# Interleaving the first two projection sections of a decoder layer by row blocks

## Chip, cores, metric

One Trainium2 chip, one core. The metric is the device time of one execution in microseconds (us), as the median of several runs. The names of the engines follow the profile: PE is TensorE (its weight loads are PEld), ACT is ScalarE, DVE is VectorE, POOL is GpSimd, SP is SyncE, which issues most of the transfers.

## What is computed

A decoder layer over 256 rows of width 1,024 in float32: a norm, one wide projection, two attention mixers, a gated merge, a feed-forward part and a last norm. The change touches the projection's first two column groups and the compression that reads them:

```python
h = rmsnorm(x, norm1_g[layer])
proj = h @ w_in[layer]
q_n = proj[..., :OFF_KV]
kv_n = proj[..., OFF_KV:OFF_GN]
...
k_c, v_c, k_s, v_s, k_w, v_w = (kv[:, :, i] for i in range(6))
...
kc = compress_blocks(k_c, cmp_pe_k[layer], cmp_k_w1[layer], cmp_k_w2[layer])
vc = compress_blocks(v_c, cmp_pe_v[layer], cmp_v_w1[layer], cmp_v_w2[layer])
...
def compress_blocks(k, pe, w1, w2):
    kb = k[:, idx] + pe[None, None, :, None, :]
    kb = jnp.transpose(kb, (0, 3, 1, 2, 4)).reshape(b, g, n_cmp, CMP_BLOCK * d)
    return jax.nn.gelu(kb @ w1) @ w2
```

The row factor of `rmsnorm` (one number for each row) is applied after the matmul, when its result is copied out of PSUM; only the gain is applied to x before it.

## The kernel before

**Weights in parts.** Each float32 matmul is made of three faster ones. A weight chunk is loaded into `raw`, ACT writes its rounded copy `whi` (`split`, line 114), DVE the remainder `wlo` (line 116); x times the gain is split the same way into `hTh` (line 187) and `hTl` (line 193). `mm3` gives the three matmuls whi x hTh, wlo x hTh and whi x hTl (all through `mm`, line 238).

**Chunks and sections.** The projection is cut into sections: kva (384 columns; chunks 0 and 1), kvb (408 columns; chunks 2 and 3), then q, qm, km and vm with 512 columns each (chunks 4 to 11), then the gates. A chunk holds four row blocks of 128 of the 1,024 rows of the weight, so a section is two chunks, eight row blocks, with two results (rows 0 to 127 and 128 to 255 of x): 48 matmuls. The pool `wp` holds three `raw`, three `whi` and three `wlo` tiles, so the load of a chunk waits until DVE has read an older one.

**Order.** The program is written in the order in which each engine executes it. `run_slot` emits a half section's matmuls; `at(pos, f, ...)` puts other work between them, at a fraction `pos` of the list. An engine works its own list strictly in order, so what is emitted earlier is also waited for first.

**The start.** kva's first chunk comes in four pieces of one row block (192 KB), three on ACT's queue and one on SP's, the second in two pieces; kvb's chunks come whole (816 KB). x comes in five pieces on SP's queue (`x_part`). A loop over the eight row blocks does `hTh`, `hTl` and `split` for kva. Then kva runs (row block by row block), and kvb after it (chunk 2: all blocks of the first result, then of the second).

**Row norm.** `row_squares` (ACT, line 204) and `row_sums` (DVE, line 207) square x and add it up near the end of kva; `row_norm` sums over partitions with four small matmuls into `tp`, DVE makes `stat` (line 213), POOL the power `rstd` (line 214). It stands in the first half of kvb, at 0.9.

**The compression's chain.** kva's results are copied out with the row factor into `kcd` and `kva` (lines 304 and 307); `cmp_gather` transposes `kcd` on PE (line 372, eight transposes) and `gather_evac` adds the positions into `kE` on DVE (line 384, eight operations), both in kvb's second half. Then follow in the q section `rope` on `kva`, `cmp_mlp1` (PE, reads `w1`), `cmp_sum` (with `gl` on ACT and DVE) and `cmp_mlp2`.

Of the kernel before, what the change touches and what calls it, by code (L numbers as in the profile page):

```python
# [8 lines left out]
F32 = mybir.dt.float32  # L9
# [36 lines left out]
def hybrid_layer(ctx: ExitStack, tc: tile.TileContext, gxd, w, w1c, small, const, gf, out):  # L46
# [39 lines left out]


    raw, hi, lo = {}, {}, {}

# [29 lines left out]


    ident = cp.tile([128, 128], F32, name="ident")
    mhalf = cp.tile([128, 4], F32, name="mhalf")
# [10 lines left out]
    gx = cp.tile([128, 16 + 2048], F32, name="gx")  # L133
    raw_tile(0)
    raw_tile(1)

# [3 lines left out]

    for k in range(3):
        load_part(0, k, 4, 1, nc.scalar)
    for a, b in ((0, 1), (1, 2), (2, 4)):
        x_part(a, b)
    load_part(0, 3, 4)
    for a in (4, 6):
        x_part(a, a + 2)
        load_part(1, a % 4, 4, 2)
    load(2)

# [10 lines left out]
    xT = gx[:, 16:].rearrange("p (k q) -> p k q", k=8)  # L161
    load(3)
    nc.sync.dma_start(sm, small)
    nc.sync.dma_start(kc_, const)
    load(4)
    g1, g2 = gx[:, 0:8], gx[:, 8:16]
# [18 lines left out]

    for kt in range(8):
        act.activation(hTh[:, kt, :], xT[:, kt, :], AF.Copy, scale=g1[:, kt:kt + 1])
        if kt == 0:
            hi[0] = wp.tile([128, 2048], F32R, name="whi")
            lo[0] = wp.tile([128, 2048], F32R, name="wlo")  # L190
            dve.tensor_copy(hi[0][:, 0:384], raw[0][:, 0:384])
            split(0, 0, 4, "l")
        dve.scalar_tensor_tensor(hTl[:, kt, :], xT[:, kt, :], g1[:, kt:kt + 1],
                                 hTh[:, kt, :].bitcast(F32), op0=ALU.mult, op1=ALU.subtract)
        if kt:
            split(kt // 4, kt % 4, 4)

    stat = cp.tile([128, 8], F32, name="stat")
    rstd = cp.tile([128, 2], F32, name="rstd")
    hrstd = stat[:, 4:6]  # L200

    def row_squares(i):
# [48 lines left out]
    def xstat(c, n, accs, kts):  # L251

        r = []
        h, l = hi[c], lo[c]
        order = [(t, k) for t in range(2) for k in range(4)]
        if c < 2:
            order.sort(key=lambda e: e[1])
        for t, k in order:
            kt = kts[k]
            if True:  # L260
                lh, ll = (a[:, kt, t * 128:(t + 1) * 128] for a in (hTh, hTl))
                r += mm3(accs[t][:, :n], lh, ll, h[:, k * n:(k + 1) * n],
                         l[:, k * n:(k + 1) * n], kt == 0, kt == 7)
        return r
# [34 lines left out]
    vm = ap_.tile([128, 2, 512], F32, name="vm")  # L299
    tm = {"kva": kva, "kvb": kvb, "vm": vm}  # L300

    def evac_tm(sec, t, acc, n):
        if sec == "kva":
            act.activation(kcd[:, t], acc[:, 0:256].rearrange("p (a d) -> p a d", a=4)[:, :, None, :]
                           .to_broadcast([128, 4, 2, 64]), AF.Copy, scale=rstd[:, t:t + 1])
            acc, n = acc[:, 256:384], 128
        act.activation(tm[sec][:, t, :], acc[:, :n], AF.Copy, scale=rstd[:, t:t + 1])
# [81 lines left out]
    def cmp_mlp1():  # L389
# [5 lines left out]
        act.activation(raw1, tp[:, 0:64], AF.Copy)  # L395
        dve.tensor_reduce(gsum, ident.rearrange("p (g i) -> p i g", g=4), op=ALU.add, axis=AX)

# [190 lines left out]
    def unit_events(s):  # L588
# [15 lines left out]
        if d > 0:  # L604
            at(0.12, d_yevac, d - 1)


    groups = [("kva", 0, 384), ("kvb", C_KVB, 408), ("q", C_Q, 512), ("qm", C_QM, 512),
              ("km", C_KM, 512), ("vm", C_VM, 512)]
    for sec, c0, n in groups:  # L610
        if sec in ("q", "qm", "km"):
            tm[sec] = ap_.tile([128, 2, 512], F32, name="qtm", bufs=2)
        if sec in ("kvb", "q"):
            accs = [ps_e.tile([128, 512], F32, name=f"{sec}acc{t}") for t in range(2)]
        else:
            accs = [acc_tile(), acc_tile()]
        for i in range(2):
            c = c0 + i
            if c == 0:
                at(0.6, load, 5)  # L620
            elif c == 1:
                at(0.88, row_squares, 0)
                for k in range(4):
                    at(0.89, split, 2, k, 4)
                for k in range(1, 4):
                    at(1.1, row_squares, k)
                at(1.1, row_sums, 0, 2, 2)
                at(1.1, row_sums, 4, 6, 2)
                at(1.1, row_sums, 0, 4, 2)
                at(1.1, row_sums, 0, 1, 1)  # L630
                for k in range(4):
                    at(1.2, split, 3, k, 4, "h")
                for k in range(2):
                    at(1.3, split, 3, k, 4, "l")

            elif c == 2:
                at(0.9, row_norm)
                for k in range(2, 4):
                    at(0.91, split, 3, k, 4, "l")
                at(0.92, load, 6)  # L640
                at(0.92, nc.sync.dma_start, w1, w1c)
            elif c == 3:
                for k in range(2):
                    at(0.0, split, 4, k, 2, "h")
                for t in range(2):
                    at(0.01, evac_tm, "kva", t, first[t], 384)
                for k in range(2):
                    at(0.1, split, 4, k, 2, "l")
                at(0.11, load, 7)
                at(0.66, cmp_gather)  # L650
                for k in range(2):
                    at(0.66, gather_evac, k)
                for k in range(2):
                    at(0.7, split, 5, k, 2, "h")
            elif c == 4:
                for t in range(2):
                    at(0.0, evac_tm, "kvb", t, second[t], 408)
                at(0.1, split, 5, 0, 2, "l")
                at(0.2, rope, kva, 2)
                at(0.3, split, 5, 1, 2, "l")  # L660
                at(0.35, load, 8)
                split_events(c, (0.5, 0.55), (0.8, 0.9))
                at(0.7, cmp_mlp1)
            else:
                std_events(c)
            unit_events(c)
            if c == 5:
                at(0.05, gate_evac)
                at(0.09, cmp_sum)
                at(0.1, transp_k, kva, tuple(a[:, 0:1] for a in kswT))  # L670
                at(0.1, rope, kvb[:, :, 0:128], 2)
                at(0.75, cmp_mlp2)
                at(0.75, transp_k, kvb[:, :, 0:128], tuple(a[:, 1:2] for a in kswT))
            if c == 6:
                at(0.45, transp_heads, tm["q"], qT, 0, 1)
                at(0.6, rope, tm["q"], 8)
# [11 lines left out]
            if c == 11:  # L688
                turn["tp"] = ["tp"]
                at(0.09, transp_heads, tm["km"], kmT, 0)  # L690
                at(0.48, transp_heads, tm["km"], kmT, 1)
            if c == 1:
                first = accs
            elif c == 3:
                second = accs
            elif i == 1:
                at(0.49 if sec == "vm" else 0.5, evac_tm, sec, 0, accs[0], n)
# [258 lines left out]
    P = {}  # L956
# [263 lines left out]
```

## Time and profile before

| | |
|---|---|
| median of the timed runs | 370.55 us (369.96, 370.55, 370.82) |
| the profiled execution | 371.17 us |
| its span (first to last instruction) | 369.4 us |
| granted PE clock | 0.998 |
| PE busy | 360.8 us, 98% of the span, 2,387 matmul records |
| DVE busy / ACT busy | 311.6 us (84%) / 234.2 us (63%) |
| transfers | 66.28 MB, 179 GB/s in the mean |

The profile is of one execution. A row of a timeline gives the start, the busy time, the engine, the line of the program, the operation, out<-in by the names of the tiles, the shape, how many were merged into the row, and in brackets how long the engine stood idle before it and what released it. A row of transfers gives the destination and source, the queue, how many, the size of each and the median time from issue to landing in us. A stretch's row gives from:to and length, then the busy time of PE, PEld, DVE, ACT and POOL with their instructions, the PE clock, the share of the DMA engines and GB/s.

### The profile page before, as it was taken

To read this page: it belongs to the slowest core of one execution; us is meant where nothing else is said; L and a number is where in the kernel's file an instruction comes from. 1 tells how busy PE (TensorE), PEld (TensorE's weight loads), DVE (VectorE), ACT (ScalarE), POOL (GpSimd) and SP (SyncE) were. 2 spreads that over 40 slices of the span, in tenths; PEclk is the share of its full clock that TensorE was granted. 3 is DMA by queue.
4 is the path that set the end of the run, shared out by engine and by line. 5 is a ranking of instruction groups with operands and counts; after the bars stand their busy time and mean duration, and the time that the engine had idled before them with its cause. 6 is when DMAs were issued, how large, how long until landed. Compare 5 with 4: busy or idle time off the path is not lost.

```text
span 369.4 us, 5952 instructions
## 1 busy us (share of the span) xinstructions
PE 360.8 (98%) x2387; PEld 318.5 (86%) x2387; DVE 311.6 (84%) x454; ACT 234.2 (63%) x353; POOL 3.7 (1%) x15
## 2 busy tenths in 40 slices
PE   8999999999999999999999999999999999999993
PEld 6987778877778888788999999999999999999983
DVE  4988879896967769766878999999999999995875
ACT  5984364757747667525465888876766677764522
POOL 1010000000000000000000000000000000000000
PEclk9999999999999999999999999999999999999999
DMA  8987436333533334533583655444565566544003
GB/s 265 398 317 295 138 111 227 114 115 114 172 148 137 115 114 137 206 115 114 178 333 119 229 227 220 171 185 184 184 213 215 227 230 227 221 177 174 0 0 114
DMA packets 11402, 66.28 MB, mean 179 GB/s; under 512 B 1264, under 2 KB 3056, under 8 KB 4080
## 3 DMA queue, kind: packets, MB, share of 16 engines
q1 hardware_dynamic: 10512, 64.55, 47.5%
q10 hardware_dynamic: 864, 1.38, 1.1%
q8 instruction: 18, 0.29, 0.3%
q14 instruction: 8, 0.07, 0.0%
HBM read 64.87 MB, written 1.05 MB: 178 GB/s over the span
## 4 chain that ended last, share of the span: by engine, by line
PE 93%; DMA 1%; ACT 1%; issue 1%; DVE 1%; SPq 0%; POOLq 0%; POOL 0%; DVEq 0%
PE acc L238 62%; PE o L238 10%; PE yb L238 6%; PE tp L238 4%; PE qacc L238 3%; PE kvbacc L238 2%; PE Sa L238 2%; PE Sa L556 1%; DMA gx<-in_gx_dram 1%; PE tp L327 1%; PE Sb L556 1%; ACT whi L114 1%; PE Sb L238 1%; PE o L843 0%; DVE wlo L116 0%
## 5 line engine op out<-in xcount | busy, mean ns | idle before, releaser
L116 DVE TENSOR_TENSOR wlo<-raw,whi 128x1024 fp32r<-128x1024 f32 (+3 forms) x85 | 109.8, 1310 | 11.2 <-ACT whi L114 11.1
L114 ACT ACTIVATE whi<-raw 128x1024 fp32r<-128x1024 f32 (+3 forms) x84 | 93.2, 1138 | 32.1 <-PE acc L238 21.8
L238 PE MATMUL acc<-h2h,whi 128*128 128x256 f32 x256 | 70.9, 277 | 0.0
L238 PE MATMUL acc<-h2l,whi 128*128 128x256 f32 x256 | 70.7, 276 | 0.0
L238 PE MATMUL acc<-h2h,wlo 128*128 128x256 f32 x256 | 70.7, 276 | 0.0
L238 PE MATMUL acc<-whi,hTh 128*128 128x512 f32 (+1 forms) x128 | 50.7, 396 | 0.3 <-ACT whi L114 0.3
L238 PE MATMUL acc<-wlo,hTh 128*128 128x512 f32 (+1 forms) x128 | 50.5, 394 | 0.1
L238 PE MATMUL acc<-whi,hTl 128*128 128x512 f32 (+1 forms) x128 | 49.4, 386 | 0.0
L238 PEld LDWEIGHTS acc<-h2l,whi 128*128 128x128 f32 x256 | 48.1, 188 | 0.0
L238 PEld LDWEIGHTS acc<-h2h,whi 128*128 128x128 f32 x256 | 48.1, 188 | 0.0
L238 PEld LDWEIGHTS acc<-h2h,wlo 128*128 128x128 f32 x256 | 48.1, 188 | 0.0
L949 ACT ACTIVATE whi<-wt 128x2048 fp32r<-128x2048 f32 x13 | 25.0, 1921 | 25.3 <-PE acc L238 24.2
L238 PEld LDWEIGHTS acc<-whi,hTh 128*128 128x128 f32 x128 | 24.3, 190 | 6.7 <-issue 1.3
L951 DVE TENSOR_TENSOR wlo<-wt,whi 128x2048 fp32r<-128x2048 f32 x13 | 29.7, 2285 | 0.1
L238 PEld LDWEIGHTS acc<-wlo,hTh 128*128 128x128 f32 x128 | 24.2, 189 | 4.6 <-DVE wlo L116 0.7
L238 PEld LDWEIGHTS acc<-whi,hTl 128*128 128x128 f32 x128 | 24.2, 189 | 4.5
L942 DVE TENSOR_TENSOR sl<-raw,sh 128x1536 fp32r<-128x1536 f32 x13 | 22.8, 1752 | 0.0
L940 ACT ACTIVATE sh<-raw 128x1536 fp32r<-128x1536 f32 x13 | 19.4, 1489 | 3.0 <-PE acc L238 3.0
L238 PE MATMUL acc<-mxl,whi 128*128 128x256 f32 x64 | 17.8, 278 | 0.0
L238 PE MATMUL acc<-mxh,wlo 128*128 128x256 f32 x64 | 17.8, 278 | 0.0
L238 PE MATMUL acc<-mxh,whi 128*128 128x256 f32 x64 | 17.7, 276 | 0.0
L901 DVE TENSOR_TENSOR al<-aq,ah 128x896 fp32r<-128x896 f32 (+1 forms) x16 | 16.2, 1011 | 0.6 <-ACT ah L899 0.6
(279 smaller groups left out, 732.7 us busy)
## 6 DMA issues: line engine op xcount, KB each, us to landing
raw<-in_ff_dram SPq DMA_DIRECT2D x32, 1024.0 KB, 4.9
raw<-in_gm_dram SPq DMA_DIRECT2D x8, 1024.0 KB, 4.8
raw<-in_wout_dram SPq DMA_DIRECT2D x4, 1024.0 KB, 4.9
raw<-in_q_dram SPq DMA_DIRECT2D x2, 1024.0 KB, 7.1
raw<-in_qm_dram SPq DMA_DIRECT2D x2, 1024.0 KB, 6.1
raw<-in_km_dram SPq DMA_DIRECT2D x2, 1024.0 KB, 5.4
raw<-in_vm_dram SPq DMA_DIRECT2D x2, 1024.0 KB, 4.8
raw<-in_upn_dram SPq DMA_DIRECT2D x2, 1024.0 KB, 5.6
```

Of the source, the lines that this page charges most:

```text
L114: act.activation(hi[c][:, a:b], raw[c][:, a:b], AF.Copy)
L116: dve.tensor_tensor(lo[c][:, a:b], raw[c][:, a:b], hi[c][:, a:b].bitcast(F32), op=ALU.subtract)
L238: pe.matmul(o, l, r, start=start, stop=stop, skip_group_check=True)
L327: pe.transpose(tp[:, j * 256 + t * 128:j * 256 + t * 128 + 128], src[:, t, (2 * i + j) * 128:(2 * i + j + 1) * 128], ident)
L556: pe.transpose(T[:, j, x, o:o + 128], P[:, 2 * x + j, c:c + 128], ident)
L901: dve.tensor_tensor(A[i][2][:, 0:b - a], aq[:, a:b], A[i][1][:, 0:b - a].bitcast(F32), op=ALU.subtract)
L940: act.activation(singles[c][0], v, AF.Copy)
L942: dve.tensor_tensor(singles[c][1], v, singles[c][0].bitcast(F32), op=ALU.subtract)
L949: act.activation(hi[c], v, AF.Copy)
L951: dve.tensor_tensor(lo[c], v, hi[c].bitcast(F32), op=ALU.subtract)
```

## The change

kva and kvb are computed in turns: for each row block, six matmuls of kva and then six of kvb, into four PSUM tiles at once. For that kvb's chunk 2 is loaded in four pieces and chunk 3 in two, in turns with kva's and x's pieces. Chunk 3 gets tiles of its own in place of a place in the pool: `raw3` (in `w1`'s memory, so `w1` is loaded later), `whi3` in two `qtm` buffers and `wlo3` in the buffers of `P` and `PT`. `Pieces` makes each of these pairs look like one tile. The loop over row blocks becomes `x_block`, with a `split` of kvb in each round; the squares and sums stand between the rounds; the row norm comes at 0.83 of the second half of the merged sections; the gather and all after it move back (the gather to the first half of q, `cmp_mlp1` and `cmp_sum` to its second, `cmp_mlp2` to qm).

```diff
+    class Pieces:
+        def __init__(self, n, tiles):
+            self.n, self.tiles = n, tiles
+        def __getitem__(self, ix):
+            j, a = divmod(ix[1].start, self.n)
+            return self.tiles[j][:, a:a + ix[1].stop - ix[1].start]
...
-    raw_tile(0)
-    raw_tile(1)
+    for c in (0, 2, 1):
+        raw_tile(c)
...
-    for k in range(3):
-        load_part(0, k, 4, 1, nc.scalar)
-    for a, b in ((0, 1), (1, 2), (2, 4)):
-        x_part(a, b)
-    load_part(0, 3, 4)
-    for a in (4, 6):
-        x_part(a, a + 2)
-        load_part(1, a % 4, 4, 2)
-    load(2)
+    load_part(0, 0, 4, 1, nc.scalar)
+    load_part(2, 0, 4, 1, nc.scalar)
+    load_part(0, 1, 4, 1, nc.scalar)
+    x_part(0, 1)
+    x_part(1, 2)
+    load_part(2, 1, 4)
+    for k in (2, 3):
+        x_part(k, k + 1)
+        load_part(0, k, 4)
+        load_part(2, k, 4)
+    raw[3] = ap_.tile([128, 2048], F32, name="raw3", tag="w1")
+    hi[3] = Pieces(816, [ap_.tile([128, 1024], F32R, name=f"whi3{j}", tag="qtm", bufs=2) for j in range(2)])
+    lo[3] = Pieces(816, [ap_.tile([128, 1536], F32R, name="wlo3" + t, tag=t) for t in ("P", "PT")])
+    for k in (4, 6):
+        x_part(k, k + 2)
+        load_part(1, k % 4, 4, 2)
+        load_part(3, k % 4, 4, 2)
+    nc.sync.dma_start(sm, small)
+    nc.sync.dma_start(kc_, const)
+    load(4)
+    load(5)
...
-    for kt in range(8):
+    def x_block(kt):
...
+    for kt in range(4):
+        x_block(kt)
+        split(2, kt, 4)
...
+    dve.tensor_reduce(gsum, ident.rearrange("p (g i) -> p i g", g=4), op=ALU.add, axis=AX)
...
-        if c < 2:
+        if c < 4:
             order.sort(key=lambda e: e[1])
...
+    first = [acc_tile(), acc_tile()]
+    second = [ps_e.tile([128, 512], F32, name=f"kvbacc{t}") for t in range(2)]
+    row_squares(0)
+    row_squares(1)
+    row_sums(0, 2, 2)
+    for k in range(4):
+        x_block(4 + k)
+        split(3, k, 4)
+        if k in (1, 2):
+            row_squares(1 + k)
+    for q in ((4, 6, 2), (0, 4, 2), (0, 1, 1)):
+        row_sums(*q)
+    load(6)
+    nc.sync.dma_start(w1, w1c)
+    for i in range(2):
+        a = xstat(i, 384, first, range(4 * i, 4 * i + 4))
+        b = xstat(2 + i, 408, second, range(4 * i, 4 * i + 4))
+        if i == 1:
+            for k in range(2):
+                at(0.5, split, 4, k, 2, "h")
+            at(0.5, split, 4, 0, 2, "l")
+            at(0.83, row_norm)
+            at(0.84, split, 4, 1, 2, "l")
+            at(0.85, load, 7)
+            for t in range(2):
+                at(0.9, kcd_evac, t, first[t])
+            for t in range(2):
+                at(0.91, kva_evac, t, first[t])
+            for k in range(2):
+                at(0.95, split, 5, k, 2, "h")
+        run_slot([m for k in range(0, 24, 6) for x in (a, b) for m in x[k:k + 6]])
...
-                at(0.66, cmp_gather)
...
             elif c == 4:
                 for t in range(2):
                     at(0.0, evac_tm, "kvb", t, second[t], 408)
-                at(0.1, split, 5, 0, 2, "l")
+                at(0.14, cmp_gather)
+                at(0.14, gather_evac, 0)
+                at(0.14, gather_evac, 1)
+                at(0.15, split, 5, 0, 2, "l")
...
-                at(0.7, cmp_mlp1)
...
             if c == 5:
                 at(0.05, gate_evac)
-                at(0.09, cmp_sum)
-                at(0.1, transp_k, kva, tuple(a[:, 0:1] for a in kswT))
+                at(0.08, cmp_mlp1)
+                at(0.08, transp_k, kva, tuple(a[:, 0:1] for a in kswT))
                 at(0.1, rope, kvb[:, :, 0:128], 2)
-                at(0.75, cmp_mlp2)
-                at(0.75, transp_k, kvb[:, :, 0:128], tuple(a[:, 1:2] for a in kswT))
+                at(0.4, cmp_sum)
             if c == 6:
+                at(0.02, cmp_mlp2)
+                at(0.02, transp_k, kvb[:, :, 0:128], tuple(a[:, 1:2] for a in kswT))
```

Three places in the engines' lists. First SP, at the start of the program (gx is x with the gains, raw a weight chunk); before:

```order
L139 DMA gx<-in_gx_dram 128x272
L139 DMA gx<-in_gx_dram 128x256
L139 DMA gx<-in_gx_dram 128x512
L96 DMA raw<-in_kva_dram 128x384
L139 DMA gx<-in_gx_dram 128x512
L96 DMA raw<-in_kva_dram 128x768
```

and now:

```order
L150 DMA gx<-in_gx_dram 128x272
L150 DMA gx<-in_gx_dram 128x256
L106 DMA raw<-in_kvb_dram 128x408
L150 DMA gx<-in_gx_dram 128x256
L106 DMA raw<-in_kva_dram 128x384
L106 DMA raw<-in_kvb_dram 128x408
L150 DMA gx<-in_gx_dram 128x256
L106 DMA raw<-in_kva_dram 128x384
```

The pieces of kvb stand between those of kva and x; on ACT's queue the second of the three pieces is now kvb's block 0 and the third kva's block 1.

Then ACT, from the last row blocks' conversions to the copies of kvb's results (kcd and kva are copies of kva's results; the whi of 1,024 columns are halves of a q chunk); before:

```order
L204 ACTIVATE xsq<-gx 128x512 x3
L114 ACTIVATE whi<-raw 128x408 x4
L114 ACTIVATE whi<-raw 128x1024 x2
L304 ACTIVATE kcd<-acc,rstd 128x512
L307 ACTIVATE kva<-acc,rstd 128x128
L304 ACTIVATE kcd<-acc,rstd 128x512
L307 ACTIVATE kva<-acc,rstd 128x128
L114 ACTIVATE whi<-raw 128x1024 x2
L307 ACTIVATE kvb<-kvbacc_274,rstd 128x408
```

and now:

```order
L206 ACTIVATE hTh<-gx 128x256
L124 ACTIVATE whi<-raw 128x384
L124 ACTIVATE whi_101<-raw_99 128x408
L124 ACTIVATE whi<-raw 128x1024 x2
L328 ACTIVATE kcd<-acc,rstd 128x512 x2
L332 ACTIVATE kva<-acc,rstd 128x128 x2
L124 ACTIVATE whi<-raw 128x1024 x2
L335 ACTIVATE kvb<-kvbacc_202,rstd 128x408
```

The first q chunk's conversions stand ahead of kcd in both; the two kcd are now next to each other.

Last DVE, around the row norm's `stat`; before:

```order
L207 TENSOR_TENSOR xsq<-xsq 128x256
L116 TENSOR_TENSOR wlo<-raw,whi 128x408 x2
L213 TENSOR_SCALAR stat<-tp 128x2
L116 TENSOR_TENSOR wlo<-raw,whi 128x408 x2
L116 TENSOR_TENSOR wlo<-raw,whi 128x1024 x2
L384 TENSOR_TENSOR kE<-tp,sm 64x2x8x15 x8
```

and now:

```order
L232 TENSOR_TENSOR xsq<-xsq 128x256
L126 TENSOR_TENSOR wlo<-raw,whi 128x1024
L238 TENSOR_SCALAR stat<-tp 128x2
L126 TENSOR_TENSOR wlo<-raw,whi 128x1024
L412 TENSOR_TENSOR kE<-tp,sm 64x2x8x15 x8
L126 TENSOR_TENSOR wlo<-raw,whi 128x1024
```

`stat` stood between remainders of kvb's last chunk; it now stands between the two remainders of the first q chunk.

More of the change, by code (lines that the diff above doesn't have):

```diff
@@ L161, in hybrid_layer @@
     xT = gx[:, 16:].rearrange("p (k q) -> p k q", k=8)
[L162 to L165, printed above, removed]
     g1, g2 = gx[:, 0:8], gx[:, 8:16]
@@ L299, in hybrid_layer, with kcd_evac, kva_evac @@
     vm = ap_.tile([128, 2, 512], F32, name="vm")
-    tm = {"kva": kva, "kvb": kvb, "vm": vm}
+    tm = {"kvb": kvb, "vm": vm}
+    def kcd_evac(t, acc):
+        act.activation(kcd[:, t], acc[:, 0:256].rearrange("p (a d) -> p a d", a=4)[:, :, None, :]
+                       .to_broadcast([128, 4, 2, 64]), AF.Copy, scale=rstd[:, t:t + 1])
+    def kva_evac(t, acc):
+        act.activation(kva[:, t, :], acc[:, 256:384], AF.Copy, scale=rstd[:, t:t + 1])
     def evac_tm(sec, t, acc, n):
[L303 to L306, printed above, removed]
         act.activation(tm[sec][:, t, :], acc[:, :n], AF.Copy, scale=rstd[:, t:t + 1])
@@ L395, in cmp_mlp1 @@
         act.activation(raw1, tp[:, 0:64], AF.Copy)
-        dve.tensor_reduce(gsum, ident.rearrange("p (g i) -> p i g", g=4), op=ALU.add, axis=AX)
     def cmp_sum():
@@ L605, in unit_events @@
             at(0.12, d_yevac, d - 1)
-    groups = [("kva", 0, 384), ("kvb", C_KVB, 408), ("q", C_Q, 512), ("qm", C_QM, 512),
-              ("km", C_KM, 512), ("vm", C_VM, 512)]
+    first = [acc_tile(), acc_tile()]
[29 more added lines that the diff above has]
+        run_slot([m for k in range(0, 24, 6) for x in (a, b) for m in x[k:k + 6]])
+    groups = [("q", C_Q, 512), ("qm", C_QM, 512), ("km", C_KM, 512), ("vm", C_VM, 512)]
     for sec, c0, n in groups:
@@ L612, in hybrid_layer @@
             tm[sec] = ap_.tile([128, 2, 512], F32, name="qtm", bufs=2)
-        if sec in ("kvb", "q"):
+        if sec == "q":
             accs = [ps_e.tile([128, 512], F32, name=f"{sec}acc{t}") for t in range(2)]
@@ L618, in hybrid_layer @@
             c = c0 + i
[L619 to L649, printed above, removed]
-                at(0.66, cmp_gather)
[L651 to L655, printed above, removed]
+            if c == 4:
                 for t in range(2):
                     at(0.0, evac_tm, "kvb", t, second[t], 408)
-                at(0.1, split, 5, 0, 2, "l")
+                at(0.14, cmp_gather)
+                at(0.14, gather_evac, 0)
+                at(0.14, gather_evac, 1)
+                at(0.15, split, 5, 0, 2, "l")
                 at(0.2, rope, kva, 2)
@@ L691, in hybrid_layer @@
                 at(0.48, transp_heads, tm["km"], kmT, 1)
[L692 to L696, printed above, removed]
+            if i == 1:
                 at(0.49 if sec == "vm" else 0.5, evac_tm, sec, 0, accs[0], n)
```

## The prediction

> **What bounds the kernel now.** I read the page first: the span and the chain of work that ended last.
>
> ```profile
> span 369.4 us, 5952 instructions
> PE 93%; DMA 1%; ACT 1%; issue 1%; DVE 1%; SPq 0%; POOLq 0%; POOL 0%; DVEq 0%
> ```
>
> TensorE (PE) sets the end: 93% of the last chain lies on it. The change adds and removes no matmul, so it can only remove or add time in which PE stands still or runs late. The view of busy time by stretches shows how much of it lies in the two sections that the change interleaves.
>
> ```profile
> 4.50:26.00 21.50, 20.51 (x110) 19.14 (x110) 17.98 (x37) 17.65 (x35) 1.19 (x2) 1.00 0.93 352
> ```
>
> From the first matmul at 4.5 us to the end of the second section PE (the first figure after the length) stands still for 21.50 - 20.51 = 1.0 us; the last columns give a full clock (1.00) and 352 GB/s. A busy matmul may still wait inside, so I read the starts in the timeline of PE.
>
> ```profile
> 7.30 0.34 PE L238 MATMUL acc<-whi,hTl 128*128 128x384 f32 x1
> 7.99 0.44 PE L238 MATMUL acc<-whi,hTh 128*128 128x384 f32 x1 [0.34 <-ACT whi L114]
> 8.58 0.45 PE L238 MATMUL acc<-wlo,hTh 128*128 128x384 f32 x1
> 8.86 0.34 PE L238 MATMUL acc<-whi,hTl 128*128 128x384 f32 x1
> 9.04 0.34 PE L238 MATMUL acc<-whi,hTh 128*128 128x384 f32 x1
> ...
> 14.76 0.34 PE L238 MATMUL kvbacc<-whi,hTh 128*128 128x408 f32 x1
> ...
> 18.67 0.34 PE L238 MATMUL kvbacc<-whi,hTh 128*128 128x408 f32 x1
> 18.86 0.50 PE L238 MATMUL tp<-ones,xsq 128*128 128x2 f32 x4
> 19.22 0.43 PE L238 MATMUL kvbacc<-wlo,hTh 128*128 128x408 f32 x1
> ...
> 22.47 0.35 PE L238 MATMUL kvbacc<-whi,hTh 128*128 128x408 f32 x1
> 22.70 0.33 PE L372 MATMUL tp<-ident,kcd 128*128 128x128 f32 x1
> 23.54 0.98 PE L372 MATMUL tp<-ident,kcd 128*128 128x128 f32 x7 [0.50 <-ACT kcd L304]
> 24.28 0.43 PE L238 MATMUL kvbacc<-wlo,hTh 128*128 128x408 f32 x1
> ```
>
> Undisturbed, a kva matmul starts every (14.76 - 9.04)/33 = 0.173 us and a kvb matmul every (18.67 - 14.76)/21 = 0.186 us. Two places are late. At row block 2 the third matmul starts at 8.86 and not at 7.30 + 3 x 0.173 = 7.82: **1.04 us** lost. At the gather, 22.47 to 24.28 is 1.81 us; less one step of 0.19 it is 1.62. Eight transposes without a wait cost 0.79 us, 43.02 - 42.23, in these rows:
>
> ```profile
> 42.23 1.03 PE L327 MATMUL tp<-ident,qtm 128*128 128x128 f32 x8
> 43.02 0.48 PE L238 MATMUL acc<-whi,hTl 128*128 128x512 f32 x1
> ```
>
> So **0.83 us** is lost at the gather. Together 1.9 us is about all that the change can win.
>
> **Term 1, the wait at the start.** Before, PE takes kva block 0, block 1, block 2; now kva 0, kvb 0, kva 1, kvb 1. The rows of ACT and of the transfers say what it waited for.
>
> ```profile
> 0.72 1.37 ACTq L96 DMA_DIRECT2D raw<-in_kva_dram  x3
> 6.94 0.51 ACT L187 ACTIVATE hTh<-gx 128x256 fp32r<-128x256 f32 x1 [1.18 <-DMA gx<-in_gx_dram]
> 7.41 0.52 ACT L114 ACTIVATE whi<-raw 128x384 fp32r<-128x384 f32 x1
> raw<-in_kva_dram ACTq DMA_DIRECT2D x3, 192.0 KB, 3.8
> raw<-in_kva_dram ACTq DMA_DIRECT2D x1, 192.0 KB, 5.7
> gx<-in_gx_dram SPq DMA_DIRECT2D x1, 128.0 KB, 3.7
> ```
>
> The three weight pieces on ACT's queue are issued from 0.72 to 2.09, the third at about 1.6. The median of the three lands 3.8 us after its issue, the third 5.7 us after: at 7.3, just before its conversion at 7.41. The x rows of block 2 came at 6.94. In the changed kernel x rows 1 land early (1.15 + 3.7 = 4.85), but kva 1 is now the **third piece on that same queue**, behind kvb 0. Ahead of it nothing is late: the matmul of 7.30 is the twelfth, so the first six end at 7.30 - 5 x 0.173 = 6.43. Piece kvb 0 (the second, 1.15 + 3.8 = 4.95) is converted in 0.52 and its remainder follows 0.59 later (8.58 - 7.99), so it is ready at 6.1, and its six matmuls end at 6.43 + 6 x 0.186 = 7.54. If kva 1 lands at 7.3, ACT converts until 7.82, PE starts at 7.87, DVE's remainder follows 0.6 later, and the second matmul starts at 8.47 and not at 7.71. Lost: 0.76, against 1.04, so term 1 is **-0.28**. Bounds: 0 (the same wait again) and -1.04 (the third piece as quick as the other two, at 5.4). I take the value near the third piece's own row. Later blocks are covered: PE needs 6 x 0.173 + 6 x 0.186 = 2.15 us for one, and its 128 + 192 + 204 = 524 KB take 1.7 us at the slower of the two rates below.
>
> ```profile
> 3.00:6.50 3.50, 3.50 (x15) 2.88 (x14) 2.29 (x5) 2.04 (x5) 0.00 (x0) 1.00 1.03 316
> 8.00:13.00 5.00, 4.85 (x26) 4.59 (x27) 4.86 (x11) 4.89 (x12) 0.00 (x0) 1.00 1.04 428
> ```
>
> The last figure is GB/s: 316 while transfers of 128 to 256 KB run, 428 when 256 to 816 KB run. [...]
>
> **Term 2, the gather's old wait.** These rows show who held it.
>
> ```profile
> 20.07 2.01 ACT L114 ACTIVATE whi<-raw 128x1024 fp32r<-128x1024 f32 x2 [2.21 <-DVE wlo L116]
> 21.98 0.67 ACT L304 ACTIVATE kcd<-acc,rstd 128x512 f32<-128x512 f32 x1
> 19.39 0.16 DVE L213 TENSOR_SCALAR stat<-tp 128x2 f32<-128x2 f32 x1 [0.38 <-PE tp L238]
> 19.64 0.97 POOL L214 TENSOR_TENSOR rstd<-stat,mhalf 128x2 f32<-128x2 f32 x1 [17.67 <-DVE stat L213]
> raw<-in_q_dram SPq DMA_DIRECT2D x1, 1024.0 KB, 7.1
> raw<-in_km_dram SPq DMA_DIRECT2D x2, 1024.0 KB, 5.4
> ```
>
> The row norm was ready at 20.61 (19.64 + 0.97), yet kcd started at 21.98, because two conversions of the first q chunk stood ahead of it in ACT's order. They began at 20.07: the chunk was issued at 12.9 and took 7.1 us, so it landed at 20.0 (DVE, named as releaser, is in the same wait; I go by the landing). With the 5.4 us of the km chunks it lands at 18.3, kcd starts at 20.65 and the gather finds it. So the 0.83 exists where that chunk is late. The change takes the gather away from there, so term 2 is **-0.83** in an execution like the profiled one and 0 where the chunk is in time.
>
> **Term 3, the gather's new wait.** The row norm moves from the first half of the second section to eight matmuls before its end. The q section now starts at 7.54 + 0.76 + 42 x 0.173 + 42 x 0.186 + 0.44 (row norm: 19.22 - 18.67, less 0.19, and 0.08 because the matmul after it takes 0.43 and not 0.35) = 23.82, where it was at 25.85. The norm's matmuls start 2 x 0.173 + 6 x 0.186 + 0.44 = 1.90 before that, at 21.92; `stat` follows 0.53 later (19.39 - 18.86) at 22.45; `rstd` ends 0.25 + 0.97 later, at 23.67. ACT has finished both q conversions (22.1 even with the chunk at 20.0), so the two kcd run at 23.7 to 24.37 and 24.3 to 24.98. PE reaches the gather after four q matmuls, at 24.73, and its second transpose reads the second kcd: it starts at 25.03 and not at 24.83, so term 3 is **+0.2**. Bounds: 0, and +1.35 (rival 2). Behind kcd in ACT's order wait the two kva copies and the second q chunk's conversions, which end at 24.98 + 0.5 + 2.0 = 27.5; PE asks for them at 23.82 + 24 x 0.23 + 0.79 = 30.1, so they are covered by 2.6 us. Behind `stat` on DVE waits the first q chunk's second remainder, done by 22.6 + 1.2 = 23.8, asked for after six q matmuls and the gather, past 26.
>
> **Term 4, DVE's queue behind the gather.** DVE begins the eight kE operations 0.58 after the second transpose (24.12 - 23.54), at about 25.6. By the time that `cmp_mlp2` needs `gl` it has to do those, five remainders of 1,024 columns, two ropes and some small ones. The rows of DVE, then of PE:
>
> ```profile
> 24.12 2.96 DVE L384 TENSOR_TENSOR kE<-tp,sm 64x240 f32<-64x240 f32 x8 [0.60 <-PE tp L372]
> 27.11 1.23 DVE L116 TENSOR_TENSOR wlo<-raw,whi 128x1024 fp32r<-128x1024 f32 x1
> 28.26 0.19 DVE L317 TENSOR_TENSOR ropa<-kva,kc 128x32 f32<-128x32 f32 x1
> ...
> 29.39 1.22 DVE L116 TENSOR_TENSOR wlo<-raw,whi 128x1024 fp32r<-128x1024 f32 x1
> 25.85 0.40 PE L238 MATMUL qacc<-whi,hTh 128*128 128x512 f32 x1
> ...
> 37.06 0.39 PE L238 MATMUL qacc<-whi,hTl 128*128 128x512 f32 x1
> ...
> 38.26 0.47 PE L238 MATMUL qacc<-whi,hTh 128*128 128x512 f32 x1
> ...
> 39.73 0.39 PE L238 MATMUL acc<-whi,hTh 128*128 128x512 f32 x1
> ```
>
> From start to start: 2.99 + 5 x 1.15 + 2 x 1.13 + some 1.6 (an estimate for kswl, the gates and the gl chain, nine short operations) = 12.6, so `gl` is there at 38.2. PE took 13.88 us for the q section (25.85 to 39.73); now the gather's 0.79 and term 3 come in, `cmp_mlp2` and the transposes beside it (38.26 - 37.06 - 0.23 = 0.97) go out to the next section, and one matmul of that is ahead, so PE asks at 23.82 + 13.88 + 0.79 + 0.2 - 0.97 + 0.23 = 37.95. Term 4 is **+0.25**, bounds 0 and +1.15 (one remainder more in the way). Everything else costs nothing: squares, sums and `gsum` lie between conversions that ACT and DVE finish before PE asks, `w1` keeps its place on SP's queue while `cmp_mlp1`, which reads it, moves back by a section, and from the qm section on the order is the old one. SP issues seven transfers more at the start (0.46 us each, 1.37/3 in ACT's row); the q chunks behind them have to wait for DVE to free the first raw tile anyway, and were issued at 12.9 before, so they lose nothing.
>
> **Sum.** -0.28 - 0.83 + 0.2 + 0.25 = -0.66. The profiled execution took 371.17 us (span 369.4 and 1.8 around it), so one like it would take 370.5. The median of the timed runs is 0.62 lower, 370.55, with runs from 369.96 to 370.82; some of them may not have had the late q chunk. I give them half of term 2: -0.24, which is **370.3 us**; with all of it 369.9, with none 370.7.
>
> **Rivals.** 1. The third piece is not late: it lands at 5.4 like its neighbours, since only the bytes beside it on SP's queue delay it, and these are fewer now (x rows come one block at a time). For it: two of three pieces took 3.8 or less; against it: the row of 5.7. Then term 1 is -1.04 and the time 370.55 - 1.04 - 0.41 + 0.45 = 369.55 (369.1 with all of term 2). 2. Slower: `stat` stands behind a remainder of the first q chunk on DVE. That remainder starts 1.15 us after the chunk lands and takes 1.22; it blocks `stat`, due at 22.45, if the chunk lands between 20.1 and 21.3. In the profile it landed at 20.0, by km's duration it would be far earlier. Then `rstd`, kcd, gather and PE are up to 1.15 later: 370.55 - 0.28 - 0.41 + 1.35 + 0.25 = 371.46. [...] 4. The turns change nothing at the start because the same place on the queue is waited for: that is most of my forecast.
>
> **Numbers.** Forecast 0.58, rival 1 0.22, rival 2 0.13, rival 3 0.07. This kernel's measurement tells about 0.2%, 0.74 us, from no change. Faster: 0.20 of rival 1 and 0.10 of the forecast (its lower end with more of term 1). Slower: 0.11 of rival 2 and 0.05 of the rest. Same: 0.54. The range goes from rival 1 with most of term 2, 369.2, to rival 2, 371.4; the forecast's own is 369.9 to 370.7.
>
> **What would show it.** Right: PE stands or is late by about 0.8 us at the first matmuls of kva block 1, near 8 us; the q section starts near 23.8; a wait of PE for kcd of some 0.2 us near 25; `cmp_mlp2` waiting for `gl` for less than 0.5 us. Wrong: no gap at 8 us (rival 1), a `stat` row that starts more than 0.3 us after the norm's matmuls end (rival 2), gaps of PE for raw pieces in blocks 2 to 7 (the cover is not there), or new waits past 45 us.

## The result and the profile after

The changed kernel takes **372.3 us** (median of 6 runs, 371.8 to 373.27), the kernel before 370.38 us beside it (6 runs, 369.96 to 370.82): a ratio of 1.0055, 95% interval 1.0038 to 1.0072, so about 2.0 us slower. Two later comparisons, on chips 4 and 8, gave 1.0023 (1.0007 to 1.004) and 1.0038 (1.0018 to 1.0058). It was forecast at 370.3, within 0.2% of before. The profiled execution of the changed kernel took 372.08 us. Its page, span and chain:

```profile
span 370.3 us, 5958 instructions
PE 90%; DMA 3%; issue 2%; ACT 2%; DVE 1%; POOL 1%; SPq 0%; POOLq 0%; DVEq 0%
```

PE's share of the chain has fallen from 93% to 90%, DMA's and ACT's have risen. The view of busy time by stretches, for the two interleaved sections (length, then PE's busy time and instructions):

```profile
4.32:23.61 19.29, 19.29 (x103) 18.92 (x102) 16.41 (x32) 13.71 (x28) 1.14 (x1) 1.00 1.01 368
```

PE is busy without a break from its first matmul to the q section, and behind the first row block none is waited for. The timeline of PE shows what a busy share hides (start, duration, engine, line, operands):

```profile
6.03 0.52 PE L263 MATMUL acc<-wlo,hTh 128*128 128x384 f32 x1
6.35 0.52 PE L263 MATMUL acc<-whi,hTl 128*128 128x384 f32 x1
6.67 0.54 PE L263 MATMUL kvbacc<-whi,hTh 128*128 128x408 f32 x1
...
8.01 0.34 PE L263 MATMUL acc<-whi,hTh 128*128 128x384 f32 x1
8.18 0.34 PE L263 MATMUL acc<-wlo,hTh 128*128 128x384 f32 x1
8.36 0.34 PE L263 MATMUL acc<-whi,hTl 128*128 128x384 f32 x1
...
23.61 0.40 PE L263 MATMUL qacc<-whi,hTh 128*128 128x512 f32 x1
...
24.31 0.39 PE L263 MATMUL qacc<-whi,hTh 128*128 128x512 f32 x1
24.86 0.33 PE L400 MATMUL tp<-ident,kcd 128*128 128x128 f32 x1 [0.16 <-ACT kcd L328]
25.44 0.98 PE L400 MATMUL tp<-ident,kcd 128*128 128x128 f32 x7 [0.25 <-ACT kcd L328]
26.17 0.48 PE L263 MATMUL qacc<-wlo,hTh 128*128 128x512 f32 x1
...
38.16 0.39 PE L263 MATMUL acc<-whi,hTh 128*128 128x512 f32 x1
38.66 0.37 PE L263 MATMUL tp<-gl,sm 64*128 64x30 f32 x2
```

Three things are to be seen. Up to 6.67 a matmul of 384 columns starts every 0.32 us, and from 8.01 every 0.17: the first ones run at half speed, and there is no gap at 8 us. The gather takes 26.17 - 24.31 = 1.86 us; less a step of 0.23 and eight transposes (0.79), **0.84 us** is lost there. `cmp_mlp2` begins 0.50 behind the matmul ahead of it; in the kernel before, where nothing is waited for there, it was 0.32 (37.06 to 37.38), so 0.18 is lost to the wait for `gl`. Who held the gather (POOL, then DVE, then ACT):

```profile
22.47 1.61 POOL L239 TENSOR_TENSOR rstd<-stat,mhalf 128x2 f32<-128x2 f32 x1 [20.50 <-DVE stat L238]
...
22.23 0.16 DVE L238 TENSOR_SCALAR stat<-tp 128x2 f32<-128x2 f32 x1
22.30 1.22 DVE L126 TENSOR_TENSOR wlo<-raw,whi 128x1024 fp32r<-128x1024 f32 x1
...
24.12 1.27 ACT L328 ACTIVATE kcd<-acc,rstd 128x512 f32<-128x512 f32 x2 [2.55 <-POOL rstd L239]
```

`stat` is on time, but the pow for `rstd` takes **1.61 us and not 0.97**: a remainder of 1,024 columns runs on DVE beside it, from 22.30 to 23.52, and the pow ends 0.56 behind that.

From the qm section on the order of work is the old one, but the time isn't: a second place far from the change costs 1.1 us. First matmul of the out projection and first transpose behind its long stretch, before:

```profile
172.16 0.28 PE L238 MATMUL acc<-mxh,whi 128*128 128x256 f32 x1
203.14 1.58 PE L843 MATMUL o<-ident,gx 128*128 128x128 f32 x13
```

and after:

```profile
171.71 0.28 PE L263 MATMUL acc<-mxh,whi 128*128 128x256 f32 x1
203.78 0.93 PE L864 MATMUL o<-ident,gx 128*128 128x128 f32 x7
```

30.98 us before and 32.07 now for the same 272 matmuls and transposes, with nothing waited for: a matmul of 256 columns starts every 118 ns and not every 113. At 171 us the changed kernel is still 0.45 us ahead, at 203 us 0.64 behind. Was that the change?

### The profile page after: what moved, and what is told of

Same layout as the page of the kernel before. It is cut to its first block, busy times and chain, and to the rows that moved or that the text cites. A ratio compares the mean times of both kernels' runs of the same rounds, so it can differ in the third digit from the quotient of the medians.

```text
span 370.3 us, 5958 instructions
## 1 busy us (share of the span) xinstructions
PE 361.9 (98%) x2387; PEld 320.2 (86%) x2387; DVE 311.5 (84%) x454; ACT 234.0 (63%) x353; POOL 4.3 (1%) x15
## 4 chain that ended last, share of the span: by engine, by line
PE 90%; DMA 3%; issue 2%; ACT 2%; DVE 1%; POOL 1%; SPq 0%; POOLq 0%; DVEq 0%
PE acc L263 61%; PE o L263 10%; PE yb L263 6%; PE tp L263 4%; DMA raw<-in_kvb_dram 3%; PE qacc L263 3%; PE Sa L263 2%; PE Sa L583 1%; PE tp L355 1%; PE Sb L583 1%; ACT whi L124 1%; PE Sb L263 1%; PE o L864 0%; DVE wlo L126 0%; POOL rstd L239 0%
## 5 line engine op out<-in xcount | busy, mean ns | idle before, releaser
L126 DVE TENSOR_TENSOR wlo<-raw,whi 128x1024 fp32r<-128x1024 f32 (+2 forms) x81 | 107.6, 1344 | 11.9 <-ACT whi L124 11.7
L124 ACT ACTIVATE whi<-raw 128x1024 fp32r<-128x1024 f32 (+2 forms) x84 | 93.3, 1138 | 31.6 <-PE acc L263 22.6
```

The costliest lines, as they stand in the source:

```text
L124: act.activation(hi[c][:, a:b], raw[c][:, a:b], AF.Copy)
L126: dve.tensor_tensor(lo[c][:, a:b], raw[c][:, a:b], hi[c][:, a:b].bitcast(F32), op=ALU.subtract)
```

## The experiments

**The same kernels again, and the pow by itself.** Two theories for the slow pace (a state that comes by chance; the buffers, which the change rotates by one), one for the pow (DVE's remainder slows it), one for the first profile of before (its late q chunk is not the rule).

> The changed kernel, unchanged, for a second profile and more times. Its first profile loses 1.10 us between 174 and 204 us, where every matmul of 256 columns takes 118 ns from start to start and not 113 as before. Theory (chance): the pace is a state that an execution falls into at the stretch's start; a second profile may show either, and the times spread by about 1 us. Rival (placement): the change moves every later chunk to another buffer of its pool, and the pace is 118 ns in every execution of the changed kernel. Under both the row norm's pow takes about 1.6 us (0.97 before) and PE loses some 0.8 us at the gather.

> The kernel before, unchanged, for a second profile. Theory: its first profile held a late first q chunk (landed at 20.0 us, gather wait 0.83 us) that most timed runs don't have; a second profile shows the chunk landed before 19 us, no wait at the gather, and a time near 370.4 and not 371.2. Rival: the chunk is late here too, and the time is near 371.2. Pace between 174 and 204 us: 113 ns if placement sets it; 113 or 118 if it is chance. Time ratio 1.000 within 0.002.

> Changed kernel, but the half of rstd is taken by DVE and not by POOL, so that DVE waits for rstd before it begins the remainder that ran beside the pow. Theory (DVE's remainder slows POOL's pow from 0.97 to 1.61 us): the pow takes about 1.0 us, kcd starts 0.6 us earlier, PE loses 0.2 us at the gather and not 0.84, and the time falls by about 0.6 us against the changed kernel. Rival (the pow is slow for another reason, or the remainder, now 1 us later, is asked for): pow 1.6 us, or a new wait of PE for the remainder near 26 us, and no gain.

```
-        pool.tensor_scalar(hrstd, rstd, 0.5, None, op0=ALU.mult)
+        dve.tensor_scalar(hrstd, rstd, 0.5, None, op0=ALU.mult)
```

> Changed kernel with a transpose into an unused bank ahead of every eighth matmul of the second and third chunk of the out projection (12 in all, 0.1 to 0.25 us each, so some 1.2 to 3 us more before any gain). Theory (a state that a disturbance ends): after a transpose the pace returns to 113 ns within some five matmuls in most of the pieces, whatever it was before. Rival (placement of the buffers): the pace between the transposes stays at 118 ns in every piece.

```
+            if i:
+                for j in range(4, 48, 8):
+                    at(j / 48, lambda: pe.transpose(bank("yb", "yb")[:, 0:128], ident, ident))
             run_slot(mms)
```

after_again 371.82 us, ratio 1.0023 (1.0007 to 1.004); before_again 370.71, ratio 0.9999 (0.998 to 1.0018); norm_quiet 370.42, ratio **0.9994** (0.9979 to 1.0009); breaks 373.48 in one run. after_again has 118 ns and a pow of 1.61 us again. The same two rows of the out projection in before_again:

```profile
171.31 0.28 PE L238 MATMUL acc<-mxh,whi 128*128 128x256 f32 x1
203.38 1.36 PE L843 MATMUL o<-ident,gx 128*128 128x128 f32 x11
```

32.07 us: the kernel before has the slow pace too, so the moved buffers are not needed for it. Its q chunk was converted from 19.32, later than the theory had it (landed before 19), and the gather lost 0.18 us (22.38 to 23.54, less 0.19 and 0.79). In breaks four of the twelve pieces went back to 113 ns and eight stayed at 118, so it is a state, but a disturbance ends it less often than was expected. The pow in norm_quiet (POOL, DVE, then PE at the gather):

```profile
22.50 0.71 POOL L239 TENSOR_TENSOR rstd<-stat,mhalf 128x2 f32<-128x2 f32 x1 [20.52 <-DVE stat L238]
...
23.25 0.17 DVE L240 TENSOR_SCALAR stat<-rstd 128x2 f32<-128x2 f32 x1 [0.83 <-POOL rstd L239]
23.32 1.22 DVE L126 TENSOR_TENSOR wlo<-raw,whi 128x1024 fp32r<-128x1024 f32 x1
...
24.34 0.39 PE L263 MATMUL qacc<-whi,hTh 128*128 128x512 f32 x1
24.57 1.03 PE L400 MATMUL tp<-ident,kcd 128*128 128x128 f32 x8
25.36 0.47 PE L263 MATMUL qacc<-wlo,hTh 128*128 128x512 f32 x1
```

With DVE waiting for `rstd`, the pow takes 0.71, the gather finds kcd ready (1.02 us from matmul to matmul, none lost), and the remainder, a microsecond later, is still in time. Against after_again the time falls by 0.29% (0.9994 / 1.0023, some 1.1 us; 0.3 to 1.9 with both intervals). The theory held. The pow fell below the 1.0 expected, so the trace shows the whole wait of 0.84 gone and not 0.6 of it; the times alone are too wide to tell these two apart.

**One part alone, and the pace taken out.** Two matmuls of 512 columns ahead of the long stretch were to settle the pace in both kernels, and one kernel has the moved row norm without the turns.

> Kernel before, with two matmuls of 512 columns into an unused bank in the middle of the first chunk of the out projection (0.45 us). Theory (the pace of the 256-column matmuls there is a state, and a stretch that follows 512-column matmuls always runs at 113 ns, as every such stretch past 205 us does in all profiles so far): from there to 203 us the pace is 113 ns, the stretch takes 30.98 + 0.45 us and not 32.08; the times come closer together. Rival: the pace stays a matter of chance, 118 ns is seen here or in the changed kernel with the same edit.

> Changed kernel with the same two matmuls. Theory: pace 113 ns, as in the kernel before with that edit, and with this lottery out of both, the difference of the two is the change's own: start -0.6, new gather wait +0.84, no old one to win, DVE's backlog +0.27, so about +0.4 us (0 to +0.8). Rival: the timed runs of the changed kernel hold a further loss that its profiles don't show, and the difference is +1.2 us or more.

```
+    def wide(c):
+        o = bank("yb", "yb")
+        for _ in range(2):
+            mm(o, hi[c][:, 0:128], hi[c][:, 0:512], True, True)
...
+            if i == 0:
+                at(0.5, wide, c)
             run_slot(mms)
```

> Kernel before with one part of the change alone: the row norm near the end of the second section, the gather and the compression behind it, each as many matmuls from the section's end as in the changed kernel; the first two sections one after the other as before. Theory (this part makes the loss, by the pow beside DVE's remainder): pow about 1.6 us, PE loses about 0.84 us at the gather and 0.27 at the second compression matmuls, the start is that of before (40th matmul near 10.9 us), time about +1.0 us against before. Rival (the turns make the loss, by shorter transfers and late pieces): no loss against before.

```
             elif c == 2:
-                at(0.9, row_norm)
...
             elif c == 3:
+                at(0.66, row_norm)
+                at(0.67, split, 4, 1, 2, "l")
...
+                    at(0.8, kcd_evac, t, first[t])
...
-                at(0.66, cmp_gather)
...
             elif c == 4:
...
+                at(0.14, cmp_gather)
```

> Changed kernel with three edits: half of rstd on DVE (as in norm_quiet), the second compression matmuls and the transposes beside them six matmuls later in the qm section, and the two 512-column matmuls. Theory: no wait for gl (0.27 less), gather wait 0.0 to 0.2, pace 113 ns: against the changed kernel with the 512-column matmuls alone 1.1 us less, against before about -1.0 us. Rival: moving the compression back only moves its wait to the first block of the km section, and less than 0.9 us is won.

```
-                at(0.02, cmp_mlp2)
+                at(0.14, cmp_mlp2)
...
-                at(0.02, transp_k, kvb[:, :, 0:128], tuple(a[:, 1:2] for a in kswT))
+                at(0.14, transp_k, kvb[:, :, 0:128], tuple(a[:, 1:2] for a in kswT))
```

before_wide 370.71, ratio 1.001 (0.9995 to 1.0025); after_wide 371.47, ratio 1.0031 (1.0018 to 1.0045); norm_only 371.43, ratio **1.0021** (1.0003 to 1.0038); quiet_late_wide 370.64, ratio 1.001 (0.9996 to 1.0025). PE in after_wide, around the wide matmuls:

```profile
174.66 0.28 PE L263 MATMUL acc<-mxh,wlo 128*128 128x256 f32 x1
174.77 0.64 PE L263 MATMUL yb<-whi 128*128 128x512 f32 x2
175.25 0.28 PE L263 MATMUL acc<-mxh,whi 128*128 128x256 f32 x1
175.37 0.28 PE L263 MATMUL acc<-mxl,whi 128*128 128x256 f32 x1
175.48 0.28 PE L263 MATMUL acc<-mxh,wlo 128*128 128x256 f32 x1
```

The pace is 118 ns ahead of them here and in before_wide, and 113 behind them in all three kernels that have them; what they cost (0.45) and win cancels in the medians. With the pace settled the changed kernel is 0.76 us above the kernel before (371.47 - 370.71), inside the theory's 0 to 0.8 and under the rival's 1.2, with an uncertainty as large as itself. quiet_late_wide missed: it lies 0.83 below after_wide, where 1.1 was expected and the rival said less than 0.9, and level with before_wide, not 1.0 below the kernel before. norm_only loses 0.8 us with the start of before and with 113 ns in its profile, so the loss comes with the moved row norm and what moves with it. Its rows are those of the changed kernel:

```profile
22.63 1.61 POOL L216 TENSOR_TENSOR rstd<-stat,mhalf 128x2 f32<-128x2 f32 x1 [20.66 <-DVE stat L215]
...
24.47 0.40 PE L240 MATMUL qacc<-whi,hTh 128*128 128x512 f32 x1
25.02 0.33 PE L381 MATMUL tp<-ident,kcd 128*128 128x128 f32 x1 [0.16 <-ACT kcd L305]
25.60 0.98 PE L381 MATMUL tp<-ident,kcd 128*128 128x128 f32 x7 [0.25 <-ACT kcd L305]
26.34 0.48 PE L240 MATMUL qacc<-wlo,hTh 128*128 128x512 f32 x1
```

**The changed stretch alone.** The whole kernel's runs spread over 3 us. Four kernels end behind the qm section, so that the time holds little else.

> Kernel before, cut off behind the qm section (all later work left out; the rows of qm and of x go out instead), so that the time holds the changed stretch and little else. A reference for the three kernels beside it. Theory (the late first q chunk of the first profile, worth 0.8 us, is not in most executions): its spans lie in a narrow group with a few some 0.8 us longer; rival: most lie at the longer end.

> Changed kernel, cut off at the same place. Theory (the loss is in this stretch: gather wait 0.84 and compression wait 0.27 in every execution, while the old gather wait and the start give back less than that in most): 0.4 to 1.0 us longer than the kernel before cut off. Rival (the mean of the profiles, 59.90, 59.17 and 59.78 us at the first score matmul before against 59.59, 59.26 and 58.85 after, holds for all executions, and the time is lost past this stretch): 0.3 us shorter.

> Kernel before with the row norm, gather and compression moved but without the turns, cut off at the same place. Theory: 0.8 to 1.1 us longer than before cut off; the turns alone (the changed kernel against this one) then gain 0 to 0.7 us. Rival: as long as before.

> Changed kernel with half of rstd on DVE and the second compression matmuls later, cut off at the same place (the edit with the 512-column matmuls lies behind the cut). Theory: 1.1 us shorter than the changed kernel cut off, 0.1 to 0.7 us shorter than before cut off. Rival (the timed kernels showed no gain against before because the turns win nothing): the same as before cut off, within 0.1 us.

```
             run_slot(xstat(c, n, accs, range(4 * i, 4 * i + 4)))
+        if sec == "qm":
+            break
...
+        nc.sync.dma_start(rows[:, 0:512], tm["qm"][:, t, :])
```

| kernel, cut off | median us | lowest to highest | runs |
|---|---|---|---|
| before_head | 58.39 | 58.17 to 58.44 | 4 |
| norm_only_head | 59.38 | 59.28 to 59.40 | 4 |
| after_head | 58.94 | 58.86 to 59.63 | 5 |
| quiet_late_head | 58.53 | 57.88 to 58.69 | 4 |

The moved row norm costs 59.38 - 58.39 = **0.99 us**, the turns win 59.38 - 58.94 = **0.44**, and together the change loses 0.55, as the theory had it (0.4 to 1.0). The kernel before lies within 0.3 us in all runs: none holds the 0.8 us of the late q chunk. Without the two new waits the changed kernel is level with before (0.14 above it), not 0.1 to 0.7 below: 0.41 us below after_head by the medians, where 1.1 was expected, and 0.98 by the two profiled runs (58.86 and 57.88). This is a miss, and the small numbers of runs don't settle by how much.

**What was still open.** The uncut kernel lost more than 0.55 us. Does the slow pace fall on it more often, and is there a version that beats both?

> Changed kernel again, for one more profile. Open is the rest of the loss: cut off behind the qm section it is 0.55 us slower than before, whole it was 0.85 and 2.0 us slower. Theory: the slow pace of the out projection (1.1 us) falls on nearly all executions of the changed kernel and on fewer of the kernel before: 118 ns here. Rival: it falls on both alike, about half each.

> Kernel before again, for one more profile. Theory (the slow pace is rarer here): 113 ns in at least one of this profile and the next; rival (both alike): no telling difference to the changed kernel, whose profiles were slow so far.

> Kernel before once more, as the run ahead of it. With the first two profiles (113 and 118 ns) this makes four draws.

> Changed kernel with half of rstd on DVE, the later compression matmuls, one 512-column matmul ahead of the out projection's long stretch in place of two, and two matmuls on a zeroed tile ahead of the warm-up transposes, so that PE works from about 0.95 us and not 1.35. Theory: the gather and compression waits are gone, the pace is 113 ns at a cost of 0.23 us, the full clock comes up to 0.4 us earlier, worth 0.1 us: 0.3 us less than quiet_late_wide, 0.3 us less than before (0.1 to 0.6). Rival: one wide matmul doesn't settle the pace (118 ns is seen), or the clock comes no earlier, and the time is that of before or above.

```
+    dve.memset(xsq[:, 0, 0:128], 0.0)
     make_identity(nc, ident)
...
+    for _ in range(2):
+        pe.matmul(warm[:, 0:128], xsq[:, 0, 0:128], xsq[:, 0, 0:128], start=True, stop=True, ...)
     for _ in range(NWARM):
```

after_p3 372.44, before_p3 370.55, before_p4 371.51 in one run each; all three have 118 ns. The unedited kernels then have 118 in three of four profiles of before and in all four of the changed kernel (after_p5, below, is the fourth). That is too few to tell whether the pace is part of the difference. early_one_wide missed: 371.66, ratio 1.0016 (0.9999 to 1.0034), the pace was 113 ns ahead of its single wide matmul and 118 behind it, and full speed came no earlier (6.61 us). The profile before_p3 shows the kernel before nearly without its waits (PE; then ACT's conversion of x block 2; then the q chunks from issue to landing):

```profile
7.38 0.34 PE L238 MATMUL acc<-whi,hTh 128*128 128x384 f32 x1
7.71 0.45 PE L238 MATMUL acc<-wlo,hTh 128*128 128x384 f32 x1
7.99 0.34 PE L238 MATMUL acc<-whi,hTl 128*128 128x384 f32 x1
...
21.60 0.35 PE L238 MATMUL kvbacc<-whi,hTh 128*128 128x408 f32 x1
21.79 1.04 PE L372 MATMUL tp<-ident,kcd 128*128 128x128 f32 x8
22.58 0.43 PE L238 MATMUL kvbacc<-wlo,hTh 128*128 128x408 f32 x1
...
6.14 0.51 ACT L187 ACTIVATE hTh<-gx 128x256 fp32r<-128x256 f32 x1 [0.41 <-DMA gx<-in_gx_dram]
...
raw<-in_q_dram SPq DMA_DIRECT2D x2, 1024.0 KB, 5.1
```

x block 2 came at 6.14 and not 6.94, the q chunk in 5.1 us and not 7.1. Row block 2 loses (7.99 - 7.38) - 2 x 0.173 = 0.26 us and not 1.04, and the gather (22.58 - 21.60 - 0.19 - 0.79) nothing; row block 1 loses 0.28, which it didn't in the first profile. before_p4 and before_head read much the same (0.31 and 0.40 us at row block 2, nothing at the gather). before_again has the late x block (6.92) and a q chunk of 6.4 us, before_wide the late x block (6.97), a q chunk of 7.0 and 0.75 lost at the gather. So three of the six profiles of before have both transfers slow and three have both quick.

> Changed kernel, unchanged, timed on the same chip as the next one. Theory (all of the loss lies in the moved row norm): 0.5 to 1.2 us slower than before, as in the first two comparisons and cut off; 118 ns in the out projection, which the kernel before shows as often.

> Changed kernel without the two new waits (half of rstd on DVE; second compression matmuls six matmuls later) and with nothing else. Theory: 1.1 us (0.84 + 0.27) less than the changed kernel on the same chip, and level with the kernel before or up to 0.4 us below it. Rival (half or more of the loss lies elsewhere, in the turns or past 55 us): no more than 0.5 us less than the changed kernel, and above the kernel before.

after_p5 371.9, ratio 1.0038 (1.0018 to 1.0058); quiet_late, with the edits of norm_quiet and of the later compression alone, 371.22, ratio 1.0015 (1.0001 to 1.0028). Between them 0.23%, some 0.85 us, with an uncertainty as large; the theory said 1.1, the rival 0.5 at most. PE shows both waits gone; the one for `gl`:

```profile
37.76 0.39 PE L263 MATMUL acc<-whi,hTh 128*128 128x512 f32 x1
38.07 0.40 PE L263 MATMUL tp<-gl,sm 64*128 64x30 f32 x2
```

0.31 from start to start, against 0.50. But quiet_late is 0.15% above before and not level or below, as the rival had it, and no version tried is clearly faster than before. norm_quiet, which still has the wait for `gl`, came out lower against before (0.9994) than quiet_late (1.0015); the waits can't explain that.

A time also holds what lies outside the span from the first to the last instruction, 1.7 to 3.0 us in these runs. The medians of the spans, which every run has, are steadier:

| | changed kernel, us | kernel before, us | difference |
|---|---|---|---|
| whole, chip 4 (12 and 29 runs) | 370.05 | 368.80 | 1.25 |
| whole, chip 8 (9 and 20 runs) | 370.10 | 368.85 | 1.25 |
| both with the two wide matmuls, chip 12 (12 and 12) | 369.40 | 368.75 | 0.65 |
| both cut off, chip 1 (5 and 4) | 57.2 | 56.6 | 0.6 |

With the pace settled the difference is that of the cut-off kernels, and half of the whole kernel's loss is gone (0.6 us, some 0.4 either way as an estimate from the runs' spread). That speaks for the slow pace falling on the changed kernel more often, as the theory of after_p3 had it, though no run shows it directly.

## Why the prediction was wrong

**"Together 1.9 us is about all that the change can win": the failed step on the side of the gain.** Both waits were read from one profile, and both hung on transfers that are slow in some executions only. In the six profiles of before the wait at the gather was 0.83, 0.75, 0.18 and three times 0; the 1.04 at row block 2 was 0.26 in before_p3. That the profiled execution lay 0.62 us above the median was seen, and half of term 2 withheld for it. The 0.41 that was counted is not far from the mean of the six, 0.29, but the four cut-off runs of before hold none of it.

**Term 3, "`rstd` ends 0.25 + 0.97 later": the failed step on the side of the cost.** Forecast +0.2, measured **+0.84**: 0.84 to 0.86 in eight of the nine profiles that have the moved row norm as it is in the change, 1.00 in after_p3. This is the largest miss of the sum. The 0.97 had been taken from a place where a remainder of 408 columns stands behind `stat`; at the new place it is one of 1,024. The pow took 0.97 or 0.98 us in all the profiles with the small one, 1.61 or 1.62 with the large one, 0.71 with none, and 1.61 - 0.97 = 0.64 is what the remainders differ by (1.22 and 0.58). DVE beside the pow in the kernel before:

```profile
19.47 1.07 DVE L116 TENSOR_TENSOR wlo<-raw,whi 128x408 fp32r<-128x408 f32 x2
```

The first of these two took 0.58 us and ended at 20.05. In both kernels the pow ended 0.56 us behind the remainder that was running when it began (20.05 to 20.61 before, 23.52 to 24.08 after). The term's upper bound of 1.35 had been drawn for another mechanism. In norm_quiet nothing runs on DVE from 22.42 to 23.25 us, and the pow takes 0.71 (22.50 to 23.21), as in the four other kernels in which DVE waits for `rstd`. So the remainder beside it costs the time; by what mechanism, no run shows.

**Term 1** was right as a mechanism in some executions only. kva 1, the third piece on ACT's queue, is waited for in after_again:

```profile
6.89 0.35 PE L263 MATMUL kvbacc<-whi,hTl 128*128 128x408 f32 x1
7.09 0.44 PE L263 MATMUL acc<-whi,hTh 128*128 128x384 f32 x1
7.68 0.44 PE L263 MATMUL acc<-wlo,hTh 128*128 128x384 f32 x1 [0.15 <-DVE wlo L126]
7.96 0.33 PE L263 MATMUL acc<-whi,hTl 128*128 128x384 f32 x1
```

(7.96 - 7.09) - 2 x 0.173 = 0.52 us, forecast 0.76. In the six profiles of the changed kernel, whole, cut off or with the wide matmuls, the loss was 0, 0, 0, 0.19, 0.52 and 1.04 (after_p3). Its conversion on ACT began between 6.03 and 6.96 us, where the prediction had the piece land at 7.3 and rival 1 at 5.4. In the first profile it began at 6.81, and no gap is seen, because the half-speed matmuls had already made PE late; in after_wide (6.03, full clock from 4.45) the piece is in time, as in rival 1. That the q section began at 23.61, forecast 23.82, is therefore luck: the slow clock took about what the wait was to take. **Term 4** was right as a mechanism: +0.18, forecast +0.25. **Rival 2** named the right sign through the wrong instruction: `stat` started 0.04 us behind the norm's matmuls (21.69 + 0.50 to 22.23), and the delay came behind it. Only in after_p3 did `stat` stand behind the remainder, by 0.16 us (22.25 to 22.45), which is the rest of its 1.00. **Rival 3**, a kva 1 that lands later, has little for it: it came earlier than forecast, and behind it no row block is waited for in any profile of the changed kernel.

For an execution with quick transfers the terms then give 0.84 + 0.18 = 1.0 for the moved row norm (0.99 measured, cut off), less what the turns win (0.44, cut off). **Open** is why the whole kernel loses more than 0.55 us: 0.8 to 2.0 in three comparisons (the lowest end of an interval 0.26), 1.25 by the spans. The excess goes when the pace is settled, which points to the pace but doesn't say why the change should bring the slow one more often. The prediction had put everything from the qm section on at nothing, because the order of work is the old one there.

## What to carry to other kernels

Read a wait from two or three profiles before pricing its removal: one that ends on a transfer may be there in one execution and not in the next (the gather's was 0.83 us in the first profile of before and 0 in three others). When a step is moved, look up what runs beside it on engines it doesn't wait for, and re-price each of its operations there. A tiny instruction on the critical chain, such as a pow of 128 by 2, can be kept clear by giving DVE something to wait for: here the pow went from 1.61 to 0.71 us (norm_quiet).

## What the runs showed of the hardware

**The full clock begins at different times.** PE works from 1.34 or 1.35 us in all profiles of both kernels, and the trace's record of the full clock began anywhere between 4.07 us (after_p3) and 7.21 (norm_quiet), 7.16 in the first profile after. Until then a matmul takes about twice as long (384 columns in the first profile after: 0.32 us from start to start, beside 0.17). Against after_again (full from 5.16) the first profile after was 0.37 us later from 11 us on. In the kernel before, the wait for x block 2 covers that: row block 3 began at 8.69 to 8.79 us with the full clock from anywhere between 4.47 and 5.65, and at 9.46 to 9.56, with the late x block, from 5.87 to 6.77. Where the changed kernel doesn't wait for kva 1 it is uncovered: its row block 2 began at 9.39, 9.81 and 10.16 with the full clock from 4.45 (after_wide), 6.23 (after_p5) and 7.16 (the first profile). From the earliest to the latest of these beginnings it is 3.1 us (4.07 to 7.21); what sets the moment wasn't found.

**Two paces for one stream.** Matmuls of 256 columns with a new weight each start every 113 or every 118 ns for 28 us on end, at the same full clock (1.00 in the first profiles before and after) and with no wait, 1.10 us apart in sum. Two 512-column matmuls ahead gave 113 ns in three of three profiles; behind a single one it went from 113 to 118 in the one profile there is; a single transpose gave 113 in four of twelve cases. What sets it wasn't found.
